# A transformer kernel on one core: PEER gate rows built for 8 tokens per operation, one conv unit less in fp32, and SBUF slots shifted by 64 bytes

## Chip, core and metric

The kernel runs as one program on one core of a Trainium2 chip. The metric is the device time of one execution in microseconds. The engines that matter are PE (TensorE, matmuls), DVE (VectorE), ACT (ScalarE), POOL (GpSimd) and SP, which issues the weight DMAs. Each has a queue of its own and works through it in order.

## What is computed

256 tokens of width 2048 pass through two blocks, everything in fp32:

```python
# first_block
z = rmsnorm(x) @ w_in                    # conv input, q, kv and k_rope latents
u = silu(layernorm(causal_depthwise_conv(a * sigmoid(g))))   # 1024 channels, 31 taps
attn = causal_attention(...)             # 8 heads
x = x + rmsnorm(concat([rmsnorm(u), rmsnorm(attn)]) @ w_out)
x = x + rmsnorm((silu(hf @ w_gate) * (hf @ w_up)) @ w_down)  # hf = rmsnorm(x), d_ff 5632
# second_block
h = x + concat([y_pool, y_lru]) @ w_out_2
zc = rmsnorm(h)
s1, s2 = scores of zc @ peer_wq against two sets of 128 keys, 8 heads
expert, gate = top 16 of the 256 sums of the two top 16, softmax   # 16384 experts
h = h + sum over the chosen experts of gate * gelu(peer_u[expert] . zc) * peer_v[expert]
out = rmsnorm(h)
```

## The kernel before

**Matmuls.** A weight matrix is streamed from HBM in pieces of [128, 2048] (tile `raw`, 3 buffers, DMA from SP). Each piece is two *parts* of 1024 columns. Of each part ACT makes `hi`, a copy rounded to fp32r (L137), and DVE makes `lo = raw - hi` (L140); both have 4 buffers. The other operand, the rows of activations, is kept as such a pair too (`lhi`/`llo`, `z2h`/`z2l`, `znh`/`znl`, `acth`/`actl`, `wsp`). Three matmuls, hi x hi, hi x low rows, lo x hi, stand for one fp32 product.

- `unit_a` (L162 to L164): the weights are stationary (128 x 128) and 256 tokens of the rows are the moving operand. A unit of 512 output columns with 16 k-tiles has 8 parts and 192 matmuls, 24 a part. Used by w_in's conv units, w_gu (22 units), half of w_in_2 (4), peer_wq (4) and peer_u (32).
- `unit_b` (L176 to L178): the rows are stationary and 512 weight columns are the moving operand; 96 matmuls a unit of 16 k-tiles. Used by w_in's q and kv, w_out, w_down (1056 matmuls), the other half of w_in_2, w_out_2. peer_v's products (L1071) have the same form.
- `unit_a32`, `unit_b32` (L186, L195): plain fp32, one matmul where the others have three, without hi and lo. A 256-column one leaves two records in the trace.

The stages run in the order w_in, w_uq and w_ukv (fp32) with attention, w_out, w_gu, w_down, w_in_2, w_out_2, peer_wq, peer_u, peer_v.

**Work between the parts.** DVE work that is not tied to the stream is put into a list, `bg`, of closures with a cost each. After the hi and lo of a part are issued and before its matmuls, `pump(opt["budget"])` takes closures from the list until their costs have used up the budget (the last may go over). `pump(1e9)` empties the list: ahead of w_out, and ahead of peer_u's unit 31. The tile framework plans the final order of each engine's queue from this order and its own estimate of times, and inserts the waits.

**Conv.** The four conv units write `upad`; each adds 62 closures (cost 440 to 473), one per tap and channel tile, to `bg` (`conv_tap`, L373 on DVE). Units 0 and 1 are fp32r, 2 and 3 fp32. Behind the taps come `conv_mean` (a column sum on PE, L225), centering, `conv_var` (a second column sum), scale, silu on ACT and `conv_out`, which writes the first 8 k-tiles of w_out's rows.

**PEER gate rows.** During peer_wq `bg` holds `scaled` (8 closures, the normalised rows znh/znl; its first add runs on POOL) and the top-16 searches; during peer_u it holds the rest of the search, the decoding, `gates` and `slots` for both halves of the tokens, and then 256 closures `token` (cost 800). `token` makes three 128-element rows on DVE: `ha` (L1006), one-hot of the first key, and `hb` (L1007, L1009), one-hot of the second key times the gate's high and low part; a matmul of the two gives the 128 x 256 gate table of the token (`gps`, PSUM, 4 buffers, two tokens each). After each second token ACT copies (L1014) and DVE adds (L1015) into `gst`; after 32 tokens POOL issues the store to `gD`. With `opt["pool"] = 3` every third `lo` of peer_wq and peer_u is made by POOL instead of DVE.

**Addresses.** Pools are laid out one behind the other in SBUF. In the program of before, modulo 128 bytes: `raw`, `hi`, `lo` at 64; the slots of `lpool` (`lhi`, `llo`, used in turn for the rows of w_in, w_out, w_gu, w_out_2 and peer_wq, and for `wsp` and `hgg`) at 64; everything behind `small` (`z2h`, `znh`, `acth`, `x32`) at 0, `kvraw` and `kvn` at 64.

Of the kernel before, what the change touches and what calls it, by code (L numbers as in the profile page):

```python
# [45 lines left out]
def build(tc, t, out, dbg=None, stop=None):  # L46

    nc = tc.nc
    dbg = dbg or {}
# [249 lines left out]
    upad = p0.tile([128, 8, 286], F32, name="upad")  # L299
# [81 lines left out]
    for u in range(4):  # L381
        opt["budget"] = 1400 if u < 2 else 2600
        pg, pa = (conv0 if u == 0 else unit_a(ps, w, xgh, xgl, 16) if u == 1 else
                  unit_a32(ps, w, lambda k: x32[k // 8][:, k % 8, :], 16))
# [4 lines left out]
        V.tensor_tensor(ua, pa, rb2, op=ALU.mult)
        V.tensor_tensor(upad[:, 2 * u:2 * u + 2, 30:], ua, sg, op=ALU.mult)  # L390
        bg.extend((440, lambda j=j: conv_first(V, j)) for j in (2 * u, 2 * u + 1))
        for k in range(1, 31):
# [54 lines left out]
    mixh, mixl = lhs()  # L447
# [238 lines left out]
    acth = p3.tile([128, 44, 256], F32R, name="acth")  # L686
    actl = p3.tile([128, 44, 256], F32R, name="actl")
# [13 lines left out]
    y = lpool.tile([128, 2, D], F32, tag="lhi", name="y3")  # L701
    x1 = lpool.tile([128, 2, D], F32, tag="llo", name="x1r")
# [31 lines left out]
    yh, yl = lhs()  # L734
# [186 lines left out]

    for c in range(2):
# [7 lines left out]
        sel = tk.tile([128, 3, 128], F32, tag="sel", name="sel")  # L930
# [54 lines left out]
        bg.append((600, slots))  # L985
# [4 lines left out]
    def open_g():  # L990
        dump("slotT", slotT)
        tkx.close()
        G["stage"] = gx.enter_context(tc.tile_pool(name="gstage", bufs=2))
        G["hot"] = gx.enter_context(tc.tile_pool(name="ghot", bufs=6))
    bg.append((0, open_g))

    def token(tok):
        j = tok % 2
        if tok % 32 == 0:
            G["st"] = G["stage"].tile([128, NK, 32], F32, tag="gst", name="gst")  # L1000
        if j == 0:
            G["ps"] = ps.tile([128, 2, 2, 128], F32, tag="tr", name="gps", bufs=4)
        a = G["hot"].tile([128, 128], F32R, tag="ha", name="ha")
        b = G["hot"].tile([128, 2, 128], F32R, tag="hb", name="hb")
        q = slice(tok, tok + 1)
        V.tensor_scalar(a, iota, slotT[:, 0, q], None, op0=ALU.is_equal)  # L1006
        V.tensor_scalar(b[:, 0, :], iota, slotT[:, 1, q], gateh[:, q].bitcast(F32),  # L1007
                        op0=ALU.is_equal, op1=ALU.mult)
        V.tensor_scalar(b[:, 1, :], iota, slotT[:, 1, q], gatel[:, q], op0=ALU.is_equal, op1=ALU.mult)  # L1009
        T.matmul(G["ps"][:, j, :, :], a, b, start=True, stop=True)  # L1010
        if j == 1:
            o = tok % 32 - 1
            g = G["st"][:, :, o:o + 2].rearrange("p i t -> p t i")
            A.activation(g, G["ps"][:, :, 0, :], AF.Copy)  # L1014
            V.tensor_tensor(g, G["ps"][:, :, 1, :], g, op=ALU.add)  # L1015
        if tok % 32 == 31:
            nc.gpsimd.dma_start(gD[tok // 32], G["st"].rearrange("p i t -> p (i t)"))
    for tok in range(S):
        bg.append((800, lambda tok=tok: token(tok)))

    opt["budget"], opt["pool"] = 1400, 3
    wsp = lpool.tile([128, 4, 4, 256], F32R, tag="lhi", name="wsp")
    hgg = lpool.tile([128, 4, 1024], F32, tag="llo", name="hgg")
# [202 lines left out]
```

## Time and profile before

| | us |
|---|---|
| median of 3 runs | 2978.49 (2977.33 to 2981.65) |
| profiled execution, its own time | 2979.55 |
| its span, first to last instruction | 2977.5 |
| PE busy | 2910.7 |
| DVE busy | 1945.5 |
| ACT busy | 1348.2 |
| POOL busy | 293.5 |

Matmuls overlap in the records: one of 256 columns is recorded with some 280 ns, while the next starts after some 120. A busy PE is therefore not a PE at its peak, and the pace is read as the length of a stretch divided by the matmuls in it. A line such as L140 is that of a helper and stands for all its callers; the tile names tell them apart.

### The profile page before, as it was taken

Reading aid. Unit: us, or ns where it says so; the run is one execution under the profiler, and the core shown is the slowest. Engines: PE = TensorE matmul, PEld = TensorE weight load, DVE = VectorE, ACT = ScalarE, POOL = GpSimd, SP = SyncE. Lnnn points to the kernel's source line nnn. Section 1 sums busy time; section 2 is a strip of 40 time slices with the busy share of each in tenths; the row PEclk is TensorE's granted clock in tenths of the full one; section 3 lists DMA queues with packets and bytes.
Section 4 is the critical chain, followed back from the end, with each engine's and each line's share of the span. In section 5 each row is a group of like instructions: output and inputs, shape, how many; then the busy total and the mean of one; then the engine's idle time right before and its main releaser. Section 6 shows DMA issues by size and latency. Waiting matters only on the chain.

```text
span 2977.5 us, 45804 instructions
## 1 busy us (share of the span) xinstructions
PE 2910.7 (98%) x18886; PEld 2655.4 (89%) x18886; DVE 1945.5 (65%) x3059; ACT 1348.2 (45%) x1629; POOL 293.5 (10%) x149
## 2 busy tenths in 40 slices
PE   8999999999999999999999999999999999999998
PEld 8887799999998888888999999999999888888886
DVE  7965655555554447856895899999434555555555
ACT  5235544444444445545444555455444444444443
POOL 0000000000000000003332222222321000000000
PEclk9999999999999999999999999999999999999999
DMA  5544555555555556465455566666867676776763
GB/s 207 178 149 141 205 191 184 184 185 184 184 206 191 196 187 220 154 216 204 178 204 207 179 231 218 216 216 221 290 225 268 234 248 240 239 243 238 247 222 141
DMA packets 120258, 615.75 MB, mean 207 GB/s; under 512 B 10321, under 2 KB 43217, under 8 KB 54769
## 3 DMA queue, kind: packets, MB, share of 16 engines
q1 hardware_dynamic: 116656, 574.16, 55.3%
q0 software_dynamic: 3392, 38.67, 3.3%
q8 instruction: 147, 2.41, 0.3%
q14 instruction: 63, 0.51, 0.1%
HBM read 570.85 MB, written 41.94 MB: 206 GB/s over the span
## 4 chain that ended last, share of the span: by engine, by line
PE 58%; issue 24%; DVE 15%; DMA 1%; ACT 1%; POOL 0%; SPq 0%; DVEq 0%; POOLq 0%; ACTq 0%
PE acc L164 12%; PE acc L163 12%; PE acc L162 12%; PE acc L178 6%; PE acc L177 6%; PE acc L176 6%; DVE lo L140 4%; DVE ha L1006 3%; PE acc L186 3%; DVE gst L1015 2%; DVE hb L1007 2%; DVE hb L1009 2%; PE acc L195 0%; DMA gD<-gst 0%; DMA hgg<-hD 0%
## 5 line engine op out<-in xcount | busy, mean ns | idle before, releaser
L140 DVE TENSOR_TENSOR lo<-raw,hi 128x1024 fp32r<-128x1024 f32 (+1 forms) x864 | 1067.9, 1237 | 885.2 <-ACT hi L137 882.9
L137 ACT ACTIVATE hi<-raw 128x1024 fp32r<-128x1024 f32 x960 | 1012.8, 1057 | 1366.9 <-PE acc L163 652.7
L164 PE MATMUL acc<-znh,lo 128*128 128x256 f32 x2048 | 572.4, 280 | 6.4 <-DVE lo L140 5.7
L162 PE MATMUL acc<-znh,hi 128*128 128x256 f32 x2048 | 572.7, 280 | 0.0
L163 PE MATMUL acc<-znl,hi 128*128 128x256 f32 x2048 | 572.5, 280 | 0.0
L1071 PE MATMUL o<-hi,wsp 128*128 128x512 f32 x2048 | 547.7, 389 | 0.0
L162 PE MATMUL acc<-lhi,hi 128*128 128x256 f32 x1792 | 508.6, 284 | 10.4 <-ACT hi L137 9.9
L163 PE MATMUL acc<-llo,hi 128*128 128x256 f32 x1792 | 508.4, 284 | 0.7 <-DVE llo L250 0.7
L164 PE MATMUL acc<-lhi,lo 128*128 128x256 f32 x1792 | 507.5, 284 | 1.1 <-DVE lo L140 1.1
L1071 PEld LDWEIGHTS o<-hi,wsp 128*128 128x128 f32 x2048 | 384.4, 188 | 79.6
L164 PEld LDWEIGHTS acc<-znh,lo 128*128 128x128 f32 x2048 | 386.2, 189 | 7.4 <-DVE lo L140 6.4
L162 PEld LDWEIGHTS acc<-znh,hi 128*128 128x128 f32 x2048 | 391.1, 191 | 0.0
L163 PEld LDWEIGHTS acc<-znl,hi 128*128 128x128 f32 x2048 | 387.0, 189 | 0.0
L162 PEld LDWEIGHTS acc<-lhi,hi 128*128 128x128 f32 x1792 | 345.1, 193 | 11.0 <-ACT hi L137 10.1
L163 PEld LDWEIGHTS acc<-llo,hi 128*128 128x128 f32 x1792 | 345.3, 193 | 1.2 <-DVE llo L250 1.2
L164 PEld LDWEIGHTS acc<-lhi,lo 128*128 128x128 f32 x1792 | 344.4, 193 | 2.0 <-DVE lo L140 1.8
L1071 PE MATMUL o<-lo,wsp 128*128 128x512 f32 x1024 | 315.4, 389 | 0.0
L140 POOL TENSOR_TENSOR lo<-raw,hi 128x1024 fp32r<-128x1024 f32 x96 | 249.1, 2595 | 607.1 <-ACT hi L137 580.9
L1071 PEld LDWEIGHTS o<-lo,wsp 128*128 128x128 f32 x1024 | 192.3, 188 | 39.8
L178 PE MATMUL acc<-hi,actl 128*128 128x512 f32 x352 | 138.7, 394 | 0.0
L177 PE MATMUL acc<-lo,acth 128*128 128x512 f32 x352 | 138.0, 392 | 0.0
L176 PE MATMUL acc<-hi,acth 128*128 128x512 f32 x352 | 136.6, 388 | 0.0
(338 smaller groups left out, 3205.4 us busy)
## 6 DMA issues: line engine op xcount, KB each, us to landing
raw<-peer_u SPq DMA_DIRECT2D x128, 1024.0 KB, 5.2
raw<-peer_v SPq DMA_DIRECT2D x128, 1024.0 KB, 5.9
raw<-w_gu SPq DMA_DIRECT2D x88, 1024.0 KB, 4.9
raw<-w_in SPq DMA_DIRECT2D x47, 1024.0 KB, 5.0
raw<-w_down SPq DMA_DIRECT2D x44, 1024.0 KB, 4.9
raw<-w_out SPq DMA_DIRECT2D x32, 1024.0 KB, 5.0
raw<-peer_wq SPq DMA_DIRECT2D x16, 1024.0 KB, 4.9
hD<-hg SPq DMA_DIRECT2D x32, 512.0 KB, 6.6
```

What stands on the lines that cost most here:

```text
L137: A.activation(hi[:, :m], raw[:, o:o + m], AF.Copy)
L140: e.tensor_tensor(lo[:, :m], raw[:, o:o + m], hi[:, :m].bitcast(F32), op=ALU.subtract)
L162: T.matmul(o, hi[:, c], xh[:, kt, :], start=(kt == 0 and m % 2 == 0), stop=False)
L163: T.matmul(o, hi[:, c], xl[:, kt, :], start=False, stop=False)
L164: T.matmul(o, lo[:, c], xh[:, kt, :], start=False, stop=(kt == nkt - 1 and m % 2 == 1))
L176: T.matmul(o, xh[:, k, s], hi, start=(kt == 0), stop=False)
L177: T.matmul(o, xh[:, k, s], lo, start=False, stop=False)
L178: T.matmul(o, xl[:, k, s], hi, start=False, stop=(kt == nkt - 1))
L186: T.matmul(acc[m // 2][:, m % 2, :], v[:, m * 128:m * 128 + 128], x(kt), start=(kt == 0 and m % 2 == 0), stop=(kt == nkt - 1 and m % 2 == 1))
L1006: V.tensor_scalar(a, iota, slotT[:, 0, q], None, op0=ALU.is_equal)
L1007: V.tensor_scalar(b[:, 0, :], iota, slotT[:, 1, q], gateh[:, q].bitcast(F32), op0=ALU.is_equal, op1=ALU.mult)
L1071: T.matmul(acc[c][o // 512 + q], x[:, s], v[:, 512 * q:512 * q + 512], start=st, stop=sp)
```

## The change

A tile of 64 bytes goes between the stream buffers and the slots. The two `lpool` slots get 4128 and 4112 elements instead of 4096, and each user takes 4096 of them from element 0 or from element 16 (64 bytes): xgh/xgl, hh/hl and peer_wq's rows from 0, the rows that are stationary operands (w_out's, w_out_2's, `wsp`) from 16. `acth` and `actl` start 16 elements into their tiles. `upad` is two columns wider. Conv unit 2 is made in fp32r with a budget of 1400. POOL makes no `lo` any more, nor the add of `scaled`. Both `slots` closures wait until the second half's gates are done and a closure of cost 4500 without work has passed. The gate rows are made for 8 tokens by four operations of 1024 elements (`hot_a`, `hot_e`, `hot_b` twice, cost 1250); the matmuls (`meet`, cost 0) and copies and adds (`store`, cost 700) of a group come one group later.

```diff
+    gap = top.enter_context(tc.tile_pool(name="gap", bufs=1)).tile([128, 16], F32, name="gap")
+    nc.vector.memset(gap, 0.0)
     lpool = top.enter_context(tc.tile_pool(name="lpool", bufs=1))
...
-    def lhs():
-        return (lpool.tile([128, 16, 256], F32R, tag="lhi", name="lhi"),
-                lpool.tile([128, 16, 256], F32R, tag="llo", name="llo"))
+    def lslot(tag, name, shape, dt=F32R, off=0):
+
+        x = lpool.tile([128, 4128 if tag == "lhi" else 4112], dt, tag=tag, name=name)[:, off:off + 4096]
...
+    def lhs(off=0):
+        return lslot("lhi", "lhi", (16, 256), off=off), lslot("llo", "llo", (16, 256), off=off)
...
-    upad = p0.tile([128, 8, 286], F32, name="upad")
+    upad = p0.tile([128, 8, 288], F32, name="upad")
...
-        opt["budget"] = 1400 if u < 2 else 2600
-        pg, pa = (conv0 if u == 0 else unit_a(ps, w, xgh, xgl, 16) if u == 1 else
+        opt["budget"] = 1400 if u < 3 else 2600
+        pg, pa = (conv0 if u == 0 else unit_a(ps, w, xgh, xgl, 16) if u < 3 else
...
-    mixh, mixl = lhs()
+    mixh, mixl = lhs(16)
...
-    acth = p3.tile([128, 44, 256], F32R, name="acth")
-    actl = p3.tile([128, 44, 256], F32R, name="actl")
+    acth, actl = (p3.tile([128, 11296], F32R, name=n)[:, 16:11280].rearrange("p (k t) -> p k t", k=44)
+                  for n in ("acth", "actl"))
...
-    yh, yl = lhs()
+    yh, yl = lhs(16)
...
-        P.tensor_tensor(z, zh[:, k:k + 2, :].bitcast(F32), zl[:, k:k + 2, :].bitcast(F32), op=ALU.add)
+        V.tensor_tensor(z, zh[:, k:k + 2, :].bitcast(F32), zl[:, k:k + 2, :].bitcast(F32), op=ALU.add)
...
-    bg.extend((1200, lambda k=k: scaled(k)) for k in range(0, 16, 2))
-
-    opt["budget"], opt["pool"] = 700, 3
+    bg.extend((2100, lambda k=k: scaled(k)) for k in range(0, 16, 2))
+
+    opt["budget"], opt["pool"] = 1100, 0
...
-        sel = tk.tile([128, 3, 128], F32, tag="sel", name="sel")
+        sel = tk.tile([128, 3, 128], F32, tag="sel", name="sel", bufs=2)
...
-        bg.append((600, slots))
+        hold.append(slots)
+        if c == 1:
+
+            bg.append((4500, lambda: None))
+            bg.append((600, hold[0]))
+            bg.append((600, hold[1]))
...
-        G["hot"] = gx.enter_context(tc.tile_pool(name="ghot", bufs=6))
+        G["hot"] = gx.enter_context(tc.tile_pool(name="ghot", bufs=2))
...
+    def hot_a(g):
+        a = G["hot"].tile([128, NT, 128], F32R, tag="ha", name="ha")
+        hot[g] = [a]
+        V.tensor_tensor(a, iota8(), over(slotT[:, 0, :], g), op=ALU.is_equal)
+
+    def hot_e(g):
+        e = G["hot"].tile([128, NT, 128], F32, tag="he", name="he")
+        hot[g].append(e)
+        V.tensor_tensor(e, iota8(), over(slotT[:, 1, :], g), op=ALU.is_equal)
+
+    def hot_b(g, i):
+        if i == 0:
+            hot[g].append(G["hot"].tile([128, NT, 2, 128], F32R, tag="hb", name="hb"))
+        x = gateh.bitcast(F32) if i == 0 else gatel
+        V.tensor_tensor(hot[g][2][:, :, i, :], hot[g][1], over(x, g), op=ALU.mult)
+
+    def meet(g, p):
+
+        a, _, b = hot[g]
+        o = ps.tile([128, 2, 2, 128], F32, tag="tr", name="gps", bufs=4)
+        for j in range(2):
+            T.matmul(o[:, j, :, :], a[:, 2 * p + j, :], b[:, 2 * p + j, :, :], start=True, stop=True)
+        hot[g, p] = o
+
+    def store(g, p):
...
+        h, l = h.rearrange("p t i -> p i t"), l.rearrange("p t i -> p i t")
+        A.activation(z, h, AF.Copy)
+        V.tensor_tensor(z, l, z, op=ALU.add)
...
+    for g in range(S // NT + 1):
+        first, last = g == 0, g == S // NT
+        for i, fn in enumerate((lambda g=g: hot_a(g), lambda g=g: hot_e(g),
+                                lambda g=g: hot_b(g, 0), lambda g=g: hot_b(g, 1))):
+            if not last:
+                bg.append((1250, fn))
+            if not first:
+                bg.append((0, lambda g=g, i=i: meet(g - 1, i)))
+                if i:
+                    bg.append((700, lambda g=g, i=i: store(g - 1, i - 1)))
+        if not first:
+            bg.append((700, lambda g=g: store(g - 1, 3)))
+
+    opt["budget"], opt["pool"] = 1400, 0
+    wsp = lslot("lhi", "wsp", (4, 4, 256), off=16)
+    hgg = lslot("llo", "hgg", (4, 1024), F32)
```

## Rows read from the trace of the kernel before

**Rows 1.** The page, busy time, share of the span and instructions of each engine

```profile
PE 2910.7 (98%) x18886; PEld 2655.4 (89%) x18886; DVE 1945.5 (65%) x3059; ACT 1348.2 (45%) x1629; POOL 293.5 (10%) x149
```

**Rows 2.** The page, chain that ended last, by engine and line

```profile
PE 58%; issue 24%; DVE 15%; DMA 1%; ACT 1%; POOL 0%; SPq 0%; DVEq 0%; POOLq 0%; ACTq 0%
```

**Rows 3.** Stretches: us, busy us (instructions) per engine, granted clock, DMA share, GB/s

```profile
61.00:115.00 54.00, 54.00 (x252) 47.54 (x251) 52.80 (x129) 3.98 (x5) 0.00 (x0) 1.00 0.42 142
400.00:880.00 480.00, 480.00 (x4003) 480.00 (x4002) 256.36 (x249) 198.50 (x209) 0.00 (x0) 1.00 0.53 183
882.00:1120.00 238.00, 238.00 (x1041) 195.29 (x1040) 112.11 (x95) 96.10 (x101) 0.00 (x0) 1.00 0.57 199
...
1263.00:1287.00 24.00, 24.00 (x211) 23.91 (x211) 15.54 (x17) 12.43 (x15) 0.00 (x0) 1.00 0.60 206
...
1592.00:1650.00 58.00, 58.00 (x495) 58.00 (x494) 27.30 (x24) 26.98 (x30) 16.05 (x7) 1.00 0.63 222
1655.00:2073.00 418.00, 395.31 (x3262) 387.41 (x3260) 418.00 (x963) 217.06 (x283) 110.81 (x49) 0.99 0.59 211
2125.00:2260.00 135.00, 135.00 (x1194) 135.00 (x1192) 42.63 (x34) 59.27 (x62) 39.35 (x17) 1.00 0.65 232
2280.00:2960.00 680.00, 680.00 (x3002) 563.25 (x3001) 372.71 (x307) 292.60 (x279) 0.00 (x0) 1.00 0.68 234
```

**Rows 4.** Timeline of DVE among the tokens: start us, us, instruction

```profile
1739.04 1.22 DVE L140 TENSOR_TENSOR lo<-raw,hi 128x1024 fp32r<-128x1024 f32 x1
...
1740.77 1.84 DVE L1006 TENSOR_SCALAR ha<-cst,slotT 128x128 fp32r<-128x128 f32 x1
...
1743.04 0.27 DVE L1006 TENSOR_SCALAR ha<-cst,slotT 128x128 fp32r<-128x128 f32 x1
...
1743.75 1.21 DVE L140 TENSOR_TENSOR lo<-raw,hi 128x1024 fp32r<-128x1024 f32 x1
1744.89 0.64 DVE L1015 TENSOR_TENSOR gst<-gps,gst 128x256 f32<-128x256 f32 x1
1745.42 0.29 DVE L1006 TENSOR_SCALAR ha<-cst,slotT 128x128 fp32r<-128x128 f32 x1
...
1748.85 1.23 DVE L140 TENSOR_TENSOR lo<-raw,hi 128x1024 fp32r<-128x1024 f32 x1
```

**Rows 5.** Waits from 1650 to 2075 us: total, times, longest

```profile
PEld gps L1010 <- DVE gst L1015: 29.5, 38, 2.3
...
PE gps L1010 <- DVE gst L1015: 21.6, 37, 2.1
```

**Rows 6.** Timeline of DVE at the end of the conv taps

```profile
182.91 3.64 DVE L373 SCALAR_TENSOR_TENSOR cu<-upad,par,cu 128x256 f32<-128x256 f32 x9
...
195.45 0.42 DVE L425 TENSOR_TENSOR rp<-acc,cs 128x256 f32<-128x256 f32 x1 [6.46 <-PE acc L186]
```

**Rows 7.** Timeline of PE: first column sum, first matmul of w_out

```profile
203.90 0.59 PE L225 MATMUL colsum<-sqc,ones 128*128 128x256 f32 x2
...
235.36 0.80 PE L176 MATMUL acc<-hi,lhi 128*128 128x512 f32 x1
```

**Rows 8.** The attention heads' stretch, columns as in rows 3

```profile
246.00:259.00 13.00, 13.00 (x32) 8.40 (x32) 4.34 (x18) 2.96 (x12) 0.00 (x0) 0.52 0.15 62
```

**Rows 9.** Timeline of POOL in the same cycle as rows 4

```profile
1739.97 2.55 POOL L140 TENSOR_TENSOR lo<-raw,hi 128x1024 fp32r<-128x1024 f32 x1 [7.29 <-ACT hi L137]
```

**Rows 10.** One line's instructions: duration min/median/max, first and last start

```profile
L958 DVE TENSOR_TENSOR one<-tabf,cst x8: 1200/1210/3315, 1516.4 to 1594.6; 128x1024 f32<-128x1024 f32 x8
```

**Rows 11.** Timeline of PE at 1522 and 1533 us

```profile
1522.14 0.38 PE L164 MATMUL acc<-znh,lo 128*128 128x256 f32 x1 [2.12 <-DVE lo L140]
...
1533.71 0.39 PE L164 MATMUL acc<-znh,lo 128*128 128x256 f32 x1 [3.57 <-DVE lo L140]
```

**Rows 12.** Timeline of DVE ahead of the second stop

```profile
1530.35 3.30 DVE L140 TENSOR_TENSOR lo<-raw,hi 128x1024 fp32r<-128x1024 f32 x1
```

More of the change, by code (lines that the diff above doesn't have):

```diff
@@ L273, in to_row @@
         return row, row[:, None, :].to_broadcast([128, 2, 256])
-    def lhs():
-        return (lpool.tile([128, 16, 256], F32R, tag="lhi", name="lhi"),
-                lpool.tile([128, 16, 256], F32R, tag="llo", name="llo"))
+    def lslot(tag, name, shape, dt=F32R, off=0):
+        x = lpool.tile([128, 4128 if tag == "lhi" else 4112], dt, tag=tag, name=name)[:, off:off + 4096]
+        k = dict(zip("abc", shape))
+        return x.rearrange("p (a b c) -> p a b c", **k) if len(shape) == 3 else x.rearrange("p (a b) -> p a b", **k)
+    def lhs(off=0):
+        return lslot("lhi", "lhi", (16, 256), off=off), lslot("llo", "llo", (16, 256), off=off)
     ps = tc.tile_pool(name="ps1", bufs=1, space=PSUM)
@@ L389, in build @@
         V.tensor_tensor(ua, pa, rb2, op=ALU.mult)
-        V.tensor_tensor(upad[:, 2 * u:2 * u + 2, 30:], ua, sg, op=ALU.mult)
+        V.tensor_tensor(upad[:, 2 * u:2 * u + 2, 30:286], ua, sg, op=ALU.mult)
         bg.extend((440, lambda j=j: conv_first(V, j)) for j in (2 * u, 2 * u + 1))
@@ L700, in build @@
     grow = p3.tile([128, D], F32, name="grow3")
-    y = lpool.tile([128, 2, D], F32, tag="lhi", name="y3")
-    x1 = lpool.tile([128, 2, D], F32, tag="llo", name="x1r")
+    y = lslot("lhi", "y3", (2, D), F32)
+    x1 = lslot("llo", "x1r", (2, D), F32)
     nc.gpsimd.dma_start(x1, x1d)
@@ L920, in build @@
                 bg.extend(top16(kq[c][:, l, :], ki[c][:, l, :], st[c][:, l, :]))
+    hold = []
     for c in range(2):
@@ L993, in open_g @@
         G["stage"] = gx.enter_context(tc.tile_pool(name="gstage", bufs=2))
-        G["hot"] = gx.enter_context(tc.tile_pool(name="ghot", bufs=6))
+        G["hot"] = gx.enter_context(tc.tile_pool(name="ghot", bufs=2))
     bg.append((0, open_g))
-    def token(tok):
-        j = tok % 2
-        if tok % 32 == 0:
-            G["st"] = G["stage"].tile([128, NK, 32], F32, tag="gst", name="gst")
[L1001 to L1023, printed above, removed]
+    NT = 8
+    hot = {}
+    def iota8():
+        return iota[:, None, :].to_broadcast([128, NT, 128])
+    def over(x, g):
+        return x[:, NT * g:NT * g + NT, None].to_broadcast([128, NT, 128])
+    def hot_a(g):
+        a = G["hot"].tile([128, NT, 128], F32R, tag="ha", name="ha")
+        hot[g] = [a]
+        V.tensor_tensor(a, iota8(), over(slotT[:, 0, :], g), op=ALU.is_equal)
@@ new lines, in store @@
+    def store(g, p):
+        o = hot.pop((g, p))
+        if g % 4 == 0 and p == 0:
+            G["st"] = G["stage"].tile([128, NK, 32], F32, tag="gst", name="gst")
+        k = NT * (g % 4) + 2 * p
+        z = G["st"][:, :, k:k + 2]
+        h, l = o[:, :, 0, :], o[:, :, 1, :]
+        h, l = h.rearrange("p t i -> p i t"), l.rearrange("p t i -> p i t")
+        A.activation(z, h, AF.Copy)
+        V.tensor_tensor(z, l, z, op=ALU.add)
+        if g % 4 == 3 and p == NT // 2 - 1:
+            nc.gpsimd.dma_start(gD[g // 4], G["st"].rearrange("p i t -> p (i t)"))
```

## The prediction

> **What bounds the kernel.** I read the page first, then the chain, then the stretches one by one. TensorE is busy 98% of the span [rows 1], and the chain of waits agrees: 58% PE, 24% "issue" (mostly PE's own stream) and 15% DVE [rows 2]. A busy share says little here, because a recorded matmul overlaps its neighbours; what counts is the pace, stretch length over matmul count, and that is in the table by stretch [rows 3]. All its rows used below for a pace have PE busy from edge to edge and a granted clock of 1.00, so neither waiting nor the clock explains a difference between them. Still the paces differ for the same 256-column matmul: 480 us / 4003 = 119.9 ns in w_gu (400 to 880), 24 / 211 = 113.7 ns in w_in_2 (1263 to 1287), 135 / 1194 = 113.1 ns late in peer_u (2125 to 2260), 58 / 495 = 117.2 ns earlier in peer_u (1592 to 1650). The 512-column matmul: 238 / 1041 = 228.6 ns in w_down, 680 / 3002 = 226.5 ns in peer_v.
>
> The second thing to see is 1655 to 2073, the 256 gate tokens: DVE is busy 418 of 418 us, and PE falls 23 us short [rows 3]. One cycle of DVE there covers three weight parts, 1739.04 to 1748.85, 9.81 us [rows 4]; PE's stops are at the gps matmuls, behind the DVE add that frees their PSUM (29.5 us on the weight load, 21.6 on the matmul, overlapping) [rows 5]. So in w_gu PE is the bound through its pace, and among the tokens DVE is.
>
> **Slots at 0 modulo 128.** By the addresses of the program of before, the moving operand lies at 64 in w_gu (lhi, llo) and at 0 in w_in_2 and peer_u (z2h, znh), with the weights at 64 in all. The new gap tile shifts lhi and llo to 0, and the slot sizes leave every later pool at 0, as it was. So w_gu (22 units of 192 matmuls, 4224), peer_wq (768) and w_in's unit 1 (192) should take the pace of the stretches at 0. That has two levels, 113.1 and 117.2, which each hold for long; the undisturbed stretches at 113 outnumber those at 117, and I weigh them 3 to 1: 114.1 ns, or 5.8 ns less. w_gu 24.4 us, peer_wq 4.4, unit 1 1.1. Bounds for w_gu: 4224 x 6.8 = 28.7 and 4224 x 2.7 = 11.4. In unit_b the rows are stationary. There acth and actl move from 0 to 64, where peer_v's wsp already is: 1056 x (228.6 - 226.5) = 2.2 us less; w_in's unit_b goes the other way, 192 x 2.1 = 0.4 more.
>
> The Trainium skill, "SBUF — State Buffer", section "Who interferes with whom", gives PE two independent read ports and says that PE never waits on anyone; by that an address would change no pace and this part would bring 0. The trace disagrees, 119.9 against 113.1 ns, but shows the address only together with the stage; so it is a rival below. "TensorE: Matmul & The Clock Gate", section "Back-to-back issue gap", gives 256 columns a gap of about 109 ns; no stretch here reaches it.
>
> **Unit 2 of the conv input.** The two fp32 units are 252 records in 54 us, 214.3 ns each [rows 3], and 128 records (two per matmul): 27.4 us a unit. As fp32r it is 192 matmuls at 114.1: 21.9, so 5.5 us less on PE. It adds 8 lo on DVE (1.14 each, 9.1 us) and 8 hi on ACT, and with a budget of 1400 instead of 2600 each of its 8 parts takes 3 conv taps instead of 6: 24 taps, 9.7 us by nine taps in 3.64 [rows 6], come later. By the costs in the code the mean of the conv is then queued five parts later. What hid this tail: the taps end at 186.6, DVE soon sits idle for 6.46 us behind PE, the first column sum runs only at 203.90, where PE's order has it, and w_out's first matmul is at 235.36 [rows 6, 7]. Five parts of 16 records are 17 us, less the 5.5 gained: the column sum comes to about 215.5. Behind it on DVE and ACT wait the centering, the second sum, the scale and the silu, about 17 us, so w_out's first rows are there at about 233 where PE could start at 230, and the other seven then arrive no faster than ACT makes them. I take 5 us lost; from below 0 (attention's matmuls fill the hole), from above 12, five parts less the gain, uncovered. A hole there also costs clock: 0.52 in the existing one at 246 to 259 [rows 8].
>
> **Gate rows.** Before, a token takes 0.71 us of DVE (1743.04 to 1743.75), an add about 0.55 (1744.89 to 1745.42), a lo 1.14 [rows 4]. A cycle of six tokens, three adds and two lo would be 8.2 us; the missing 1.6 is the ha that takes 1.84 while POOL's lo runs (2.55 us) [rows 4, 9]. Per eight tokens (four parts) that is 9.81 x 4/3 = 13.08 us. After: four operations of 1024 elements (the same shape, also with broadcast inputs, L958, has a median of 1210 ns [rows 10], as a lo's 1.22, so 1.13 from start to start), four adds and now four lo: 4.5 + 2.2 + 4.6 = 11.3 us. The adds walk their elements in another order; at the 0.70 of the slower ones it would be 11.9. PE needs 104 matmuls: 12.2 us at 117.2, 11.8 at 113.1. The costs in the code give four parts per group, (1250, 1250), (700, 1250), (700, 1250), (700, 700), so two tokens a part as before, and the tokens end seven parts earlier, with no rest to pump before unit 31. So PE becomes the bound by a small margin: (13.08 - 12.2) x 32 = 28 us gained. I take 117.2, since gps matmuls still break the stream; 113.1 would give 42, DVE at 11.9 with small waits about 20.
>
> The lo that POOL made go to DVE. Where DVE was late without tokens, PE stood 2.12 and 3.57 us, the second on a lo stretched to 3.30 [rows 11, 12]: 5.7 us go with POOL's share, and POOL, with its lo gone, issues the eight gD stores no later than before. In peer_wq, scaled gets a third operation of 512 elements on DVE: three of about 0.6 and a lo are 2.9 us a part against 24 x 114.1 = 2.74 on PE, for 8 parts 1.5 us. The memset, the second sel buffer and the later slots cost nothing: they stand before the first weights arrive or in 1592 to 1650, where DVE is busy 27 of 58 us [rows 3]. upad's two columns move kvn, which 128 fp32 records stream; a pace changed by 2.7 ns would be 0.3 us.
>
> **Sum.** 24.4 + 4.4 + 1.1 + 2.2 - 0.4 + 5.5 - 5 + 28 + 5.7 - 1.5 = 64.4 us. The profiled execution took 2979.55 us, 2 us of it around the span of 2977.5, and lies 1 us over the median of the runs, 2978.49; so 2979.55 - 64.4 = 2915.
>
> **Rivals.**
> A. Pace at 117.2 in w_gu and peer_wq: 11.4 + 2.1 + 0.5 for 29.9, so 16 us worse: 2931. For it: 1592 to 1650 stays there undisturbed. Against: w_in_2 and the last 135 us of peer_u.
> B. 113.1 everywhere, tokens too: 5 more in w_gu and peer_wq, 14 in the tokens, the conv tail hidden 5, some 3 in the rest of peer_u, 27 in all: 2888.
> C. The address does nothing and the pace belongs to the stage: the 31.7 us of pace fall away, and unit 2 gives 1.1 less: 2948. Against: by DVE's load, the other thing that differs, the stretches don't sort (65% at 113.7 ns, 53% at 119.9, 32% at 113.1) [rows 3]. The Trainium skill's port rule, above, would have it this way.
> D. DVE stays the bound among the tokens, by adds that wait in its order: the 28 shrink to 5 or so: 2938.
> E. Slower side: the gst add. DVE works in order, and an add placed ahead of the next lo waits for a gps matmul that stands behind a whole part on PE, 24 x 117.2 = 2.8 us. Once per group: 11.3 + 2.8 = 14.1 us, 33 us over before's 418, against 36 gained elsewhere: no change, 2976. Twice: 16.9, 122 over, 3065. It decides at a period of about 14.2 us. Against: before has no idle time of DVE ahead of its adds [rows 4], the order being planned around them.
>
> **Chances and range.** Forecast 0.50, A 0.15, B 0.12, C 0.08, D 0.10, E 0.05. Leaving out E, part of C and the end of B: 2887 to 2946. About 0.2% (6 us) is what a measurement of this kernel can tell from no change: faster 0.95, same 0.02, slower 0.03.
>
> **What would show it.** In w_gu, length over count of 113 to 117 ns instead of 120, in w_down 226.5. From the first hot operation to the last gst about 390 us with PE without gaps at gps, POOL without lo. A column sum near 215 and a gap of a few us ahead of w_out. Wrong would be a pace of 120 at the new address, waits of DVE for gps ahead of gst, or a gap of over 12 us before w_out.

## The result and the profile after

The changed kernel takes 2948.49 us (median of 4 runs, 2947.42 to 2949.90), the kernel before beside it 2979.22 (4 runs, 2977.33 to 2981.65): a ratio of 0.9897, 95% interval 0.9880 to 0.9914. It is faster, by 31 us where 64 were forecast, and its time lies 2.5 us above the range. The profiled execution took 2947.42 us, its span is 2945.6.

Busy time per engine and the chain of the changed kernel, against [rows 1, 2]:

```profile
PE 2905.0 (99%) x18950; PEld 2640.4 (90%) x18950; DVE 1899.1 (64%) x2532; ACT 1326.9 (45%) x1638; POOL 28.4 (1%) x45
...
PE 71%; issue 25%; DVE 3%; ACT 1%; DMA 0%; POOL 0%; SPq 0%; DVEq 0%; POOLq 0%; ACTq 0%
```

DVE's share of the chain went from 15% to 3%: the tokens no longer wait for it. PE is now the bound nearly everywhere, so the pace (length of a stretch over its matmuls) decides. The same stretches as in [rows 3, 8], columns as there:

```profile
246.00:259.00 13.00, 13.00 (x52) 10.13 (x51) 8.71 (x16) 11.38 (x21) 0.00 (x0) 0.90 0.00 1
...
400.00:860.00 460.00, 460.00 (x3908) 460.00 (x3907) 249.94 (x243) 193.07 (x203) 0.00 (x0) 1.00 0.54 187
880.00:1110.00 230.00, 230.00 (x996) 187.92 (x994) 105.83 (x89) 92.45 (x97) 0.00 (x0) 1.00 0.55 190
1370.00:1460.00 90.00, 90.00 (x771) 90.00 (x770) 86.38 (x268) 42.30 (x51) 2.20 (x4) 1.00 0.52 179
1640.00:1990.00 350.00, 350.00 (x2970) 350.00 (x2969) 302.71 (x344) 169.87 (x257) 3.75 (x7) 1.00 0.65 236
2010.00:2210.00 200.00, 200.00 (x1701) 200.00 (x1700) 93.15 (x77) 86.79 (x91) 0.00 (x0) 1.00 0.67 236
2230.00:2920.00 690.00, 690.00 (x2970) 559.42 (x2970) 370.48 (x306) 290.89 (x278) 0.00 (x0) 1.00 0.67 231
```

Length over count: w_gu 117.7 ns (119.9 before), w_down 230.9 (228.6), the tokens 117.8 without a gap on PE, the rest of peer_u 117.6 (113.1), peer_v 232.3 (226.5). So three of these stretches got slower matmuls, and peer_v with its 3072 is the costly one: 3072 x 5.8 ns = 18 us. Nothing in the prediction expects that.

The stages, worked out from the starts in the trace (first matmul of a stage to the first of the next, peer_v to its last matmul), in us, for this kernel and the experiments below. The first column runs from w_in through w_out. The experiments did not run beside the changed kernel; a difference to it is one of medians, and by the ratios to the kernel before, which ran beside each, it comes out 1 to 2 us otherwise.

| | w_in to w_out | w_gu | w_down | w_in_2, w_out_2 | peer_wq | peer_u | peer_v |
|---|---|---|---|---|---|---|---|
| before | 359.8 | 512.2 | 250.2 | 244.5 | 103.0 | 790.0 | 696.1 |
| changed | 354.7 | 502.1 | 252.6 | 247.0 | 99.0 | 755.0 | 713.6 |
| e1, addresses as before | 355.1 | 512.0 | 250.2 | 244.5 | 100.7 | 755.0 | 696.1 |
| e2, addresses alone | 360.6 | 502.1 | 252.6 | 247.0 | 101.7 | 791.5 | 713.6 |
| e3, stationary rows at 192 | 353.9 | 502.1 | 247.9 | 245.2 | 99.0 | 755.0 | 696.1 |
| e4, and moving rows at 128 | 350.8 | 483.5 | 247.9 | 245.5 | 95.9 | 757.5 | 696.1 |
| e5, conv unit 2 undone | 362.1 | 502.1 | 252.5 | 247.0 | 99.0 | 755.0 | 713.6 |
| e6, POOL's part back | 354.9 | 502.1 | 252.6 | 247.0 | 103.5 | 761.2 | 713.6 |
| e7, e4 and `ha` at 192 | 352.7 | 484.3 | 247.9 | 244.5 | 96.1 | 734.5 | 696.1 |

The rows of work that changed beside the pace. DVE among the tokens, one group of eight, against [rows 4]:

```profile
1759.42 1.23 DVE L1025 TENSOR_TENSOR ha<-cst,slotT 128x1024 fp32r<-128x1024 f32 x1 [0.77 <-PE gps L1043]
...
1763.97 0.42 DVE L1055 TENSOR_TENSOR gst<-gps,gst 128x256 f32<-128x256 f32 x1
1764.30 1.22 DVE L1030 TENSOR_TENSOR he<-cst,slotT 128x1024 f32<-128x1024 f32 x1
1765.44 2.35 DVE L143 TENSOR_TENSOR lo<-raw,hi 128x1024 fp32r<-128x1024 f32 x2
...
1769.35 1.23 DVE L143 TENSOR_TENSOR lo<-raw,hi 128x1024 fp32r<-128x1024 f32 x1 [0.90 <-ACT hi L140]
...
1771.69 1.23 DVE L1025 TENSOR_TENSOR ha<-cst,slotT 128x1024 fp32r<-128x1024 f32 x1 [0.77 <-PE gps L1043]
```

From one `ha` to the next are 12.27 us, forecast 12.2; DVE now rests inside it (0.77 us behind PE's gps, 0.90 behind ACT's hi), and an add takes 0.42 us where before it took 0.64. From the first of these operations (1610.33) to the last add (2001.49) are 391 us, forecast about 390. No wait of PE for DVE like [rows 5] is left between 1640 and 2000. The conv tail on PE, against [rows 7]:

```profile
216.26 0.59 PE L228 MATMUL colsum<-sqc,ones 128*128 128x256 f32 x2
...
244.84 0.50 PE L179 MATMUL acc<-hi,lhi 128*128 128x512 f32 x1 [2.08 <-ACT lhi L491]
```

The first column sum came at 216.26, forecast about 215.5, and there is a gap of 2.08 us ahead of w_out's first product.

### The profile page after: what moved, and what is told of

It reads as the page before. It is cut to its first block, busy times and chain, and to the rows that moved or that the text cites. A ratio compares the mean times of both kernels' runs of the same rounds, so it can differ in the third digit from the quotient of the medians.

```text
span 2945.6 us, 45194 instructions
## 1 busy us (share of the span) xinstructions
PE 2905.0 (99%) x18950; PEld 2640.4 (90%) x18950; DVE 1899.1 (64%) x2532; ACT 1326.9 (45%) x1638; POOL 28.4 (1%) x45
## 4 chain that ended last, share of the span: by engine, by line
PE 71%; issue 25%; DVE 3%; ACT 1%; DMA 0%; POOL 0%; SPq 0%; DVEq 0%; POOLq 0%; ACTq 0%
PE acc L167 16%; PE acc L165 16%; PE acc L166 16%; PE acc L180 6%; PE acc L181 6%; PE acc L179 6%; PE acc L189 2%; PE gps L1043 1%; DVE lo L143 1%; PE acc L198 0%; ACT junk L656 0%; PE yp L838 0%; PE scp L922 0%; PE sp L515 0%; DMA raw<-w_in 0%
## 5 line engine op out<-in xcount | busy, mean ns | idle before, releaser
L143 DVE TENSOR_TENSOR lo<-raw,hi 128x1024 fp32r<-128x1024 f32 (+1 forms) x968 | 1177.1, 1219 | 904.5 <-ACT hi L140 902.7
L140 ACT ACTIVATE hi<-raw 128x1024 fp32r<-128x1024 f32 (+1 forms) x968 | 1021.6, 1057 | 1403.2 <-PE acc L166 716.0
L1122 PE MATMUL o<-hi,wsp 128*128 128x512 f32 x2048 | 559.3, 395 | 0.0
L165 PE MATMUL acc<-lhi,hi 128*128 128x256 f32 x1856 | 522.5, 282 | 10.5 <-ACT hi L140 9.5
L167 PE MATMUL acc<-lhi,lo 128*128 128x256 f32 x1856 | 522.5, 283 | 1.2 <-DVE lo L143 1.2
L166 PE MATMUL acc<-llo,hi 128*128 128x256 f32 x1856 | 518.7, 280 | 0.9 <-DVE llo L253 0.9
L166 PEld LDWEIGHTS acc<-llo,hi 128*128 128x128 f32 x1856 | 351.6, 189 | 1.4 <-DVE llo L253 1.4
L180 PE MATMUL acc<-lo,lhi 128*128 128x512 f32 (+1 forms) x352 | 137.2, 390 | 0.0
## 6 DMA issues: line engine op xcount, KB each, us to landing
hD<-hg SPq DMA_DIRECT2D x32, 512.0 KB, 3.2
```

What stands on the lines that cost most here:

```text
L140: A.activation(hi[:, :m], raw[:, o:o + m], AF.Copy)
L143: e.tensor_tensor(lo[:, :m], raw[:, o:o + m], hi[:, :m].bitcast(F32), op=ALU.subtract)
L165: T.matmul(o, hi[:, c], xh[:, kt, :], start=(kt == 0 and m % 2 == 0), stop=False)
L166: T.matmul(o, hi[:, c], xl[:, kt, :], start=False, stop=False)
L167: T.matmul(o, lo[:, c], xh[:, kt, :], start=False, stop=(kt == nkt - 1 and m % 2 == 1))
L180: T.matmul(o, xh[:, k, s], lo, start=False, stop=False)
```

## The experiments

Theory 1: for each form of matmul the pace hangs on where the rows lie relative to the weights, modulo 256 bytes and not 128. By the addresses in the programs, weights at 192 modulo 256 in both kernels, the kernel before had w_gu's and `wsp`'s rows at 192 too and `znh`, `z2h`, `acth` at 128. The changed one has `lhi` at 0 and `llo` at 128 for moving rows, `acth` at 192, `actl` at 64, and `wsp` at 64: a step of 128 for peer_v, which modulo 128 is none. (These addresses are read from the programs that the kernels build; no row of a profile has them.) The rival (Theory 2): the address part is a gain as forecast, and peer_v is slower for another reason.

**e1, the addresses undone.**

```diff
-    gap = top.enter_context(...)
-    nc.vector.memset(gap, 0.0)
...
-    def lslot(tag, name, shape, dt=F32R, off=0):
...
+    def lhs():
+        return (lpool.tile([128, 16, 256], F32R, tag="lhi", name="lhi"),
+                lpool.tile([128, 16, 256], F32R, tag="llo", name="llo"))
...
-    upad = p0.tile([128, 8, 288], F32, name="upad")
+    upad = p0.tile([128, 8, 286], F32, name="upad")
...
+    acth = p3.tile([128, 44, 256], F32R, name="acth")
+    actl = p3.tile([128, 44, 256], F32R, name="actl")
...
-    wsp = lslot("lhi", "wsp", (4, 4, 256), off=16)
+    wsp = lpool.tile([128, 4, 4, 256], F32R, tag="lhi", name="wsp")
```

> The changed kernel with every address edit undone (no gap tile, slots, act buffers and upad as in the kernel before); gate rows, conv unit 2 as fp32r and POOL's share stay as changed. Theory 1 (the new addresses are a net loss: stationary rows lose 5.9 ns per 512-column matmul, moving rows win only 2.2 ns per 256-column matmul): peer_v at 226.5 ns (696 us instead of 714), w_out and w_out_2 about 5 us shorter each, w_down 229, w_gu and peer_wq back at 120 ns (512 and 103 us); total about 15 us under the changed kernel, 2933. Theory 2 (the address part is a gain, as predicted, and peer_v's slower pace has another cause, such as the tokens or POOL's share): peer_v stays at 232 ns and w_gu goes to 120; total 2960 or more.

Measured: 2936.52 us (4 runs, 2935.48 to 2937.04), 0.9860 of before (0.9841 to 0.9879), 12 us under the changed kernel. w_gu and peer_v, columns as above:

```profile
400.00:870.00 470.00, 470.00 (x3919) 470.00 (x3918) 251.33 (x244) 193.50 (x203) 0.00 (x0) 1.00 0.54 183
...
2235.00:2915.00 680.00, 680.00 (x3002) 563.06 (x3001) 374.74 (x309) 293.69 (x280) 0.00 (x0) 1.00 0.68 235
```

119.9 and 226.5 ns: both as before, with tokens and POOL as changed. Theory 2 fails: the address edits cost the changed kernel time. Two sizes expected came smaller: w_in_2 with w_out_2 got 2.5 us shorter, where 5 were expected of w_out_2 alone, and peer_wq came to 100.7 us instead of 103.

**e2, the addresses alone,** the same lines put into the kernel before, and nothing else.

> The kernel before with the address edits alone. Theory 1: w_gu and peer_wq at 117.8 ns (about 14 us gained), peer_v and both w_out at 232 ns (about 29 us lost): 15 us slower than before, about 2994. Theory 2: peer_v stays at 226.5 ns, w_gu at 118 or below: 14 to 30 us faster, 2950 to 2965. Rival C of the prediction (address does nothing): no change, 2979.

Measured: 2993.43 us (5 runs, 2988.95 to 2998.43), 1.0053 of before (1.0033 to 1.0072): 13.9 us slower than the 2979.52 beside it.

```profile
400.00:860.00 460.00, 460.00 (x3908) 460.00 (x3907) 250.97 (x245) 194.06 (x205) 0.00 (x0) 1.00 0.55 187
...
2275.00:2970.00 695.00, 695.00 (x2993) 563.49 (x2992) 373.10 (x308) 292.67 (x279) 0.00 (x0) 1.00 0.66 229
```

117.7 ns in w_gu and 232.2 in peer_v, with per-token rows and POOL's lo. The prediction's rival C (the address does nothing) falls too.

The Trainium skill, "SBUF — State Buffer", section "Who interferes with whom", gives PE's two reads ports of their own, independent of each other, which let equal paces be expected. The measurement decides against equal paces, by 13.9 us here and, with no other engine at work, by 113.3 against 120.0 ns in the two runs that follow; whether the ports are the reason, no run here shows.

**micro_addr and micro_weights, the pace by itself.** The loops of `unit_a` and `unit_b` on slices of fixed tiles, 192 or 96 matmuls each, a stop between them; one run of each.

```diff
+    def cols(res):
+        return [w[:, (768 + res) // 4:(768 + res) // 4 + 1024] for w in W]
+    def rows(res):
+        return [z[:, res // 4:res // 4 + 4096].rearrange("p (k t) -> p k t", k=16) for z in X]
```

> Leaves out the whole computation: only matmuls run, on constant data, with no other engine at work, 192 of 256 columns (weights stationary, rows moving) and 96 of 512 columns (rows stationary, weights moving) in each segment, in the kernel's order of operands; weights stay at 192 modulo 256 bytes, the rows' address goes through 0, 64 ... 448 modulo 512, up and down again. Theory 1: the pace at 512 columns is 226.5 ns where rows and weights agree modulo 256 (192 and 448) and about 232 elsewhere, at least at 64; the pace at 256 columns is 120 at 192 and 448 and 113 to 118 at 0 and 128. Theory 2 (it is work of other engines, not the address): one pace per shape at all eight addresses, with the same scatter up and down.

> Leaves out the whole computation: only matmuls on constant data, with no other engine at work. First the 256-column form (weights stationary) and the 512-column form (rows stationary) with weights at 0, 64, 128 and 192 modulo 256 bytes and rows at the same four: 16 pairs each. Theory R (the difference of the two addresses counts): the pairs with one difference share one pace. Theory S (each operand's own address counts): the fast column of rows, 128 at 256 columns, is the same for all weights. Then twelve segments with weights at 192 and rows at 128, in the middle of which two gate-row matmuls (256 columns, other tiles) stand, at six pairs of addresses of their own. Theory L (a matmul of other tiles shifts the stream into a slower rhythm that holds until TensorE next stops): 113.3 ns before them and 117.8 behind, for some pairs or all. Rival (the slower level among the tokens comes from DVE, ACT and the DMAs): 113.3 on both sides.

Measured, from the 10th to the 150th start of a stretch (256 columns) and the 6th to the 70th (512 columns), by the rows' address minus that of the weights, modulo 256:

| rows minus weights | 0 | 64 | 128 | 192 |
|---|---|---|---|---|
| 256 columns, rows moving, ns | 120.0 | 117.8 | 118.7 | 113.3 |
| 512 columns, rows stationary, ns | 226.7 | 233.3 | 232.4 | 228.9 |

In micro_addr the eight addresses give these values twice over, upwards and downwards, to 0.1 ns, and 256 to 448 repeat 0 to 192. In micro_weights 30 of the 32 pairs of addresses give the value of their difference, to 0.4 ns. The two others: weights 64, rows 0, at 256 columns 117.8 instead of 113.3; weights 128, rows 0, at 512 columns 233.3 instead of 232.4. So Theory R, the difference, holds, and S, the rows' own address, falls. Four 256-column stretches of equal length of micro_weights, weights at 192, rows at 0, 64, 128 and 192 in turn (a count includes the two or three that lie over an edge):

```profile
316.00:330.00 14.00, 14.00 (x122) 14.00 (x121) 0.00 (x0) 0.00 (x0) 0.00 (x0) 1.00 0.01 1
339.00:353.00 14.00, 14.00 (x121) 14.00 (x120) 0.00 (x0) 0.00 (x0) 0.00 (x0) 1.00 0.00 1
362.00:376.00 14.00, 14.00 (x126) 14.00 (x125) 0.00 (x0) 0.00 (x0) 0.00 (x0) 1.00 0.00 1
384.00:398.00 14.00, 14.00 (x119) 14.00 (x119) 0.00 (x0) 0.00 (x0) 0.00 (x0) 1.00 0.01 1
```

DVE and POOL are at 0.00, the clock at 1.00: 126 matmuls fit where 119 to 122 did. The best difference is not the same for the two forms: 192 where the rows move, 0 where they are stationary. For weights at 192 the moving form came as expected: 117.8 and 113.3 ns with the rows at 0 and 128, 120.0 at 192. In the stationary form about 232 ns were expected wherever rows and weights differ; rows at 128 gave 228.9.

The table sorts the kernel's stages. Before: w_gu difference 0, 119.9 ns; z2 and zn 192, 113.1 to 113.7; `wsp` 0, 226.5; `acth` 192, 228.6. Changed: `wsp` 128, 232.3. Where a stage mixes two differences, as the changed w_gu (64 and 192, 117.7 ns) and w_down (0 and 128, 230.9), the table has no value for it.

The gate-row part of micro_weights: two matmuls of other tiles in the middle of a stream at 113.3 ns. With stationary and moving operand at (128, 128), (192, 192), (128, 192) and (0, 0) the next 28 steps have a mean of 117.6 to 117.9 ns; at (192, 128) it stays at 113.4; at (64, 64) the first seven steps have 115.6, and from there on it is back at 113.3. The second round of six repeats that. First (128, 128), then (192, 128) on PE:

```profile
790.34 0.28 PE L68 MATMUL acc<-xl,wh 128*128 128x256 f32 x1
790.45 0.28 PE L69 MATMUL acc<-xh,wl 128*128 128x256 f32 x1
790.57 0.40 PE L56 MATMUL gps<-ha 128*128 128x256 f32 x2
790.80 0.28 PE L67 MATMUL acc<-xh,wh 128*128 128x256 f32 x1
790.92 0.28 PE L68 MATMUL acc<-xl,wh 128*128 128x256 f32 x1
791.04 0.28 PE L69 MATMUL acc<-xh,wl 128*128 128x256 f32 x1
791.16 0.28 PE L67 MATMUL acc<-xh,wh 128*128 128x256 f32 x1
791.28 0.28 PE L68 MATMUL acc<-xl,wh 128*128 128x256 f32 x1
...
836.13 0.28 PE L67 MATMUL acc<-xh,wh 128*128 128x256 f32 x1
836.25 0.28 PE L68 MATMUL acc<-xl,wh 128*128 128x256 f32 x1
836.36 0.28 PE L69 MATMUL acc<-xh,wl 128*128 128x256 f32 x1
836.47 0.28 PE L67 MATMUL acc<-xh,wh 128*128 128x256 f32 x1
836.59 0.28 PE L68 MATMUL acc<-xl,wh 128*128 128x256 f32 x1
```

Four steps behind the first take 0.48 us, behind the second 0.46; over 28 steps that is 117.8 and 113.4 ns. So the same stream has two paces that each hold, called rhythms from here on, and Theory L holds here, with no other engine at work. The changed kernel shows the same at its first gate-row matmul, whose operands both lie at 128:

```profile
1624.08 0.28 PE L165 MATMUL acc<-znh,hi 128*128 128x256 f32 x1
...
1624.76 1.12 PE L1043 MATMUL gps<-hb,ha 128*128 128x256 f32 x8
1625.72 0.28 PE L165 MATMUL acc<-znh,hi 128*128 128x256 f32 x1
...
1626.31 0.28 PE L167 MATMUL acc<-znh,lo 128*128 128x256 f32 x1
```

Six steps ahead of it take 0.68 us, 113 ns; five behind it 0.59 us, 118 ns. From there the pace is 117.8 until peer_v, 220 us past the last token; no two starts on the way lie more than 0.26 us apart.

The gate-row matmuls are not the only ones that do this. In the kernel before, the pace changes at the two `slp` matmuls at 1586.86 us (they belong to `slots`), 66 us ahead of its first gate-row matmul:

```profile
1585.83 0.28 PE L162 MATMUL acc<-znh,hi 128*128 128x256 f32 x1
...
1586.74 0.28 PE L164 MATMUL acc<-znh,lo 128*128 128x256 f32 x1
1586.86 0.38 PE L980 MATMUL slp<-cst,sel 128*128 128x128 f32 x2
...
1587.19 0.28 PE L163 MATMUL acc<-znl,hi 128*128 128x256 f32 x1
...
1588.37 0.28 PE L164 MATMUL acc<-znh,lo 128*128 128x256 f32 x1
```

Eight steps ahead take 0.91 us, ten behind 1.18. So the 58 us from 1592 on in [rows 3], the prediction's source for 117.2 and rival A's evidence, are the slower rhythm and not undisturbed; from 2117 to the end of peer_u it is the faster one, behind a short stop at 2116.17. What sets the rhythm is not the pair of addresses alone: the `slp` operands lie at (128, 128) in the kernel before, the changed one and e4, and in the changed kernel the stream stays at 113.3 behind them, in e4 it goes from 117.8 back to 113.3.

**e3, the stationary rows at 192,** the weights' own place; the moving rows stay. The gap tile is left out, and each user's offset in its slot does its work.

```diff
-        x = lpool.tile([128, 4128 if tag == "lhi" else 4112], dt, tag=tag, name=name)[:, off:off + 4096]
+        off = (16 if moving else 0) if tag == "lhi" else (32 if moving else 48)
+        x = lpool.tile([128, 4112 if tag == "lhi" else 4144], dt, tag=tag, name=name)[:, off:off + 4096]
...
-    acth, actl = (p3.tile([128, 11296], F32R, name=n)[:, 16:11280]...
+    acth = p3.tile([128, 11296], F32R, name="acth")[:, 16:11280].rearrange("p (k t) -> p k t", k=44)
+    actl = p3.tile([128, 11312], F32R, name="actl")[:, 48:11312].rearrange("p (k t) -> p k t", k=44)
```

> The changed kernel with the moving rows (w_in, w_gu, peer_wq) and everything behind the slots at its addresses, but the stationary rows (w_out, w_down, w_out_2, peer_v) at 192 modulo 256 bytes, as the weights are, instead of at 64 or 192 by buffer. Theory 1 (what counts for stationary rows is the residue modulo 256 beside that of the weights): peer_v and both w_out at 226.5 ns, w_down at 226.5 to 229, w_gu and peer_wq as in the changed kernel: 25 us under the changed kernel, about 2922. Theory 2 (peer_v's pace does not hang on its rows' address): peer_v stays at 232 ns, total within 4 us of the changed kernel.

Measured: 2922.87 us (5 runs, 2922.62 to 2924.41), 0.9816 of before (0.9801 to 0.9832), 25.6 us under the changed kernel. w_down and peer_v:

```profile
880.00:1100.00 220.00, 220.00 (x972) 182.21 (x972) 103.42 (x87) 89.43 (x93) 0.00 (x0) 1.00 0.57 195
...
2220.00:2900.00 680.00, 680.00 (x3002) 563.25 (x3001) 374.95 (x309) 293.68 (x281) 0.00 (x0) 1.00 0.68 236
```

226.3 and 226.5 ns: w_down runs faster than in either kernel. peer_v gives 17.5 of the 25.6 us, w_down 4.7.

**e4, and the moving rows at 128,** both buffers, difference 192.

```diff
-        off = (16 if moving else 0) if tag == "lhi" else (32 if moving else 48)
-        x = lpool.tile([128, 4112 if tag == "lhi" else 4144], dt, tag=tag, name=name)[:, off:off + 4096]
+        off = (48 if moving else 0) if tag == "lhi" else (0 if moving else 16)
+        x = lpool.tile([128, 4144 if tag == "lhi" else 4112], dt, tag=tag, name=name)[:, off:off + 4096]
```

> As the run with the stationary rows at 192 modulo 256, and the moving rows of w_in, w_gu and peer_wq moved as well, both buffers to 128 modulo 256, where w_in_2 and peer_u have theirs (in the changed kernel one is at 0 and one at 128). Theory (both moving buffers at 128 give the lower of the two paces, 113.3 ns): w_gu 502 to about 484 us, peer_wq 99 to 96.5, w_in's units 1 and 2 about 1.3 less: 20 us under that run, about 2903. Rival (in w_gu and peer_wq the pace of 117.8 comes from the load or the rhythm of the stage, not from the buffer at 0): no change, 2923.

Measured: 2900.76 us (5 runs, 2900.20 to 2901.75), 0.9732 of before (0.9718 to 0.9746). w_gu, then the tokens:

```profile
380.00:840.00 460.00, 460.00 (x4061) 460.00 (x4060) 258.14 (x254) 202.64 (x212) 0.00 (x0) 1.00 0.57 195
...
1610.00:1960.00 350.00, 350.00 (x2970) 350.00 (x2969) 303.60 (x345) 169.48 (x257) 3.75 (x7) 1.00 0.64 236
```

113.3 ns in w_gu, the faster of the two levels that the prediction weighed for it and put down to 0 modulo 128. The tokens stay at 117.8.

**e7, `ha` at 192 as well.**

```diff
-        a = G["hot"].tile([128, NT, 128], F32R, tag="ha", name="ha")
+        o = 0 if g % 2 else 16
+        a = G["hot"].tile([128, 1040], F32R, tag="ha", name="ha")[:, o:o + 1024].rearrange("p (t i) -> p t i", t=NT)
...
-        e = G["hot"].tile([128, NT, 128], F32, tag="he", name="he")
+        e = G["hot"].tile([128, 1040], F32, tag="he", name="he")[:, :1024].rearrange("p (t i) -> p t i", t=NT)
```

> The run with moving rows at 128 and stationary rows at 192, and beside that the stationary operand of the gate-row matmuls, ha, moved from 128 to 192 modulo 256 bytes (hb stays at 128), the pair that left the rhythm alone when matmuls ran by themselves. Theory L (the gate-row matmuls shift the stream into the slower rhythm, which holds from the first of them to peer_v): the 594 us from there to peer_v's start go from 117.8 to 113.3 ns, less what DVE holds up at a period of 11.3 to 11.8 us per eight tokens: 15 to 23 us less, 2878 to 2886. Rival (other engines' work among the tokens makes the level): no change, 2901.

Measured: 2877.89 us (5 runs, 2873.88 to 2879.49), 0.9655 of before (0.9638 to 0.9671). The tokens, then the rest of peer_u:

```profile
1610.00:1950.00 340.00, 340.00 (x3002) 340.00 (x3002) 306.64 (x350) 171.20 (x259) 3.74 (x7) 1.00 0.66 247
...
1970.00:2165.00 195.00, 195.00 (x1723) 195.00 (x1722) 93.81 (x79) 87.81 (x92) 0.00 (x0) 1.00 0.69 243
```

113.3 and 113.2 ns. 64 bytes in the place of one small operand took 23 us off peer_u, in stretches where DVE, ACT and the DMAs do what they did in e4; the rival falls. This version beats both kernels.

**e5, conv unit 2 in fp32 again,** and **e6, POOL's part again.**

```diff
-        opt["budget"] = 1400 if u < 3 else 2600
-        pg, pa = (conv0 if u == 0 else unit_a(ps, w, xgh, xgl, 16) if u < 3 else
+        opt["budget"] = 1400 if u < 2 else 2600
+        pg, pa = (conv0 if u == 0 else unit_a(ps, w, xgh, xgl, 16) if u == 1 else
```

> The changed kernel with unit 2 of the conv input in fp32 again, as before. Theory (the edit is worth what the stretch up to w_uq shows, 7 us, hardly any of it lost to a late conv tail): 6 us slower than the changed kernel, 2954. The prediction's term (5.5 gained on TensorE, 5 lost behind the later conv taps): no more than 1 us of difference, 2949.

```diff
-        V.tensor_tensor(z, zh[:, k:k + 2, :].bitcast(F32), zl[:, k:k + 2, :].bitcast(F32), op=ALU.add)
+        P.tensor_tensor(z, zh[:, k:k + 2, :].bitcast(F32), zl[:, k:k + 2, :].bitcast(F32), op=ALU.add)
...
-    bg.extend((2100, lambda k=k: scaled(k)) for k in range(0, 16, 2))
+    bg.extend((1200, lambda k=k: scaled(k)) for k in range(0, 16, 2))
...
-    opt["budget"], opt["pool"] = 1100, 0
+    opt["budget"], opt["pool"] = 700, 3
...
-    opt["budget"], opt["pool"] = 1400, 0
+    opt["budget"], opt["pool"] = 1400, 3
```

> The changed kernel with POOL's part in peer_wq and peer_u restored: scaled's first add and every third lo on POOL, with the costs and budgets of before; the gate rows stay at eight tokens per operation. The prediction's terms (5.7 us of stalls on POOL's lo outside the tokens, less 1.5 for scaled): 4 us slower than the changed kernel, 2953. Rival (with the tokens cheap on DVE, POOL's lo again collide with them on the way to PE): stops of PE among the tokens, 10 to 20 us slower. Other rival (POOL's share does no harm once DVE has room): 2948.

Measured: e5 2954.48 us (4 runs, 2953.48 to 2955.02; 0.9911 of before, 0.9894 to 0.9927), 6.0 over the changed kernel; e6 2960.16 (5 runs, 2958.30 to 2962.56; 0.9932, 0.9918 to 0.9947), 11.7 over it. By the ratios the differences are 0.0014 and 0.0035 of 2980, 4 and 10 us, and the stages bear them out: 7.4 us up to w_gu for e5, 4.5 in peer_wq and 6.2 in peer_u for e6. e6 in peer_wq and among the tokens:

```profile
1370.00:1465.00 95.00, 91.72 (x775) 90.90 (x774) 86.34 (x263) 41.90 (x51) 40.04 (x22) 1.00 0.49 174
...
1660.00:2030.00 370.00, 370.00 (x3139) 370.00 (x3139) 314.01 (x323) 180.11 (x273) 115.86 (x48) 1.00 0.63 235
```

The tokens run at 117.9 ns without a gap with POOL's lo among them, so e6's first rival, stops there, is wrong: what POOL's part costs lies in peer_wq, where PE stands 3.3 of 95 us, and in the search ahead of the tokens, where PE waits 6.0 us for DVE (4.2 for `lo`, 1.8 at the first `gps`) against 1.7 in the changed kernel.

## Why the prediction was wrong

**The step that failed is "Slots at 0 modulo 128".** It gave 24.4 + 4.4 + 1.1 + 2.2 - 0.4 = 31.7 us to the address edits; measured alone they cost 13.9 (e2), undone they give back 12.0 (e1). The step went wrong in three places. It read addresses modulo 128, and alone, where their distance from the weights modulo 256 counts; so peer_v, whose rows "already" were at 64, got no term, and lost 17.5 us. It let w_gu take the pace of w_in_2 and peer_u because both would be 0 modulo 128; w_gu, with two thirds of its matmuls at a difference of 64, came to 117.7, near the 117.2 of rival A, and gave 10.1 instead of 24.4 us, peer_wq 1.7 instead of 4.4 by e1. The two levels that the step weighed 3 to 1 are two rhythms at one difference, 192, and w_gu did not have that difference. And acth and actl at 64 modulo 128 were to gain 2.2 in w_down and lost 2.4, w_in_2 with w_out_2 another 2.5. The trace of before held differences 0 and 192 only. Differences of 64 and 128 are not among [rows 3], and the bounds, 28.7 and 11.4, had no loss in them; the other end should have been one, and for peer_v too.

**Gate rows, right in the number.** Forecast were 28 us at a period of 12.2; e6, which has this part without POOL's, is 28.8 us under before in peer_u, and the period of the changed kernel is 12.27. That PE would be the bound at 117.2 ns was right as a number; the reason given, a broken stream, was too loose: by e7 it is the place of the gate-row matmuls' operands that shifts the stream in the changed kernel, and the shift stays until peer_v, where the prediction let the pace return to 113.1 after the tokens. So the match is in part luck: the last 152 us of peer_u ran at 113.3 before, and at 117.8 they take some 6 us more (an estimate from the two paces), which the rest of the stage made good.

**POOL's share, too small.** 5.7 - 1.5 = 4.2 forecast, 10 to 12 measured. The third operation of `scaled` was to lose 1.5 in peer_wq; the stage gained 4.5 of e6's 103.5, and with POOL's lo PE stands in it (e6): [rows 11, 12] were taken for all of POOL's stalls, and they are those of peer_u alone.

**Conv unit 2, too small.** 0.5 forecast, 4 to 7 measured. The gain on PE (5.5) was about right: w_in's first matmul behind the conv units starts at 110.12 us, in e5 at 115.27. So was the path of the tail: the column sum at 216.26, the gap of 2.08 us, w_out's first product 9.5 us later than in [rows 7]. But it cost nothing, the lower bound given: the hole of [rows 8], 32 matmuls at a clock of 0.52 (31 at 0.50 in e5), was filled with 52 at 0.90.

**Rivals.** D and E did not come: DVE has no idle time ahead of its adds among the tokens. C falls by e2; that its sum, 2948, is the time measured is luck: the addresses cost 13.9 us, and the other parts, 46.5 us where 32.7 were forecast, happened to bring that in. B's 113 ns in w_gu and among the tokens came only with e4 and e7. A was near on w_gu (11.4 forecast, 10.1 measured) and peer_wq (2.1, 1.7). Worked out from single parts, 28.8 + 11.7 + 6.0 - 13.9 = 32.6 us against 30.7 measured.

## What to carry to other kernels

Where a stream of matmuls is the bound, take the pace per stage, length over count, and sort it by the distance of the two operands' SBUF addresses modulo 256 bytes, not by one address; a table of all four distances for each form costs one small run, and a distance that the trace doesn't hold can be a loss as well as a gain. The values are those of these two forms in these runs. Pad each tile for the role that it has: in this kernel moving rows 64 bytes below the weights' place and stationary rows on it, also the small operands of a matmul that only visits the stream. A whole group of edits that ends faster can hold one that is a loss: here leaving the addresses alone would have given 12 us more, choosing them by the table gave 48 (e4), and the place of `ha` another 23 (e7).

## What was not expected of the hardware

With no other engine at work, TensorE at a granted clock of 1.00 showed four steady paces per form, by the distance of its operands in SBUF modulo 256 bytes: 113.3 to 120.0 ns at 256 columns, 226.7 to 233.3 at 512. At a distance of 192 the 256-column stream has two rhythms, 113.3 and 117.8 ns; two matmuls of other tiles can shift it from the first to the second, and with their operands at (192, 128) they did not. In the changed kernel the second rhythm lasted from 1624.76 us to peer_v. Short stops of PE change it too, either way: from 113.3 to 117.8 behind a step of 0.68 us at 1514.83 (e4), back to 113.3 behind one of 0.34 us at 2116.17 (before). Why a distance has its pace, what decides which rhythm a stream takes, and why the pair at weights 64 and rows 0 ran at 117.8, these runs do not show.
